# A decoder step on one core: single-group pairs as two chains of two in PSUM, and the gmlp operands stored unsplit

## The chip, the cores and the metric

The kernel runs on one core of a Trainium2 chip. The metric is the device time of one execution in microseconds (us). The engines are TensorE (PE in the profile), VectorE (DVE), ScalarE (ACT), GpSimd (POOL) and SyncE (SP). Here SP issues all loads and stores of data, in the order in which they stand in its program.

## The reference

One layer of a hybrid decoder trunk, for a sample group of 8 sequences of 8 tokens and a prompt of 1024 tokens, which share the weights (D_MODEL 1024, D_FF 2816, float32):

```
h = rmsnorm(x, norm_mix)
q, k, v, gu, gv, ga, gb = split(h @ w_in)
o  = sliding-window attention of 128 with sinks          # sample: cached keys and values
vn = layernorm(gelu(gv));  s = gelu(gu) * (tril(W_s[g]) @ vn + b[g])   # 6 groups of 128 channels
merged = sigmoid(ga) * (o @ w_pa) + sigmoid(gb) * (s @ w_pb)
x = x + merged @ w_out
z = rmsnorm(x, norm_ffn) @ w_up;  c = causal conv of width 3 over z
x = x + (gelu(c_a) * c_b) @ w_down;  y = rmsnorm(x, norm_final)
```

## The kernel before

**Tiling.** Tokens lie on the free axis, in two groups: g0 has the 64 sample tokens and 512 of the prompt (576), g1 the other 512. A float32 value is kept as a high and a low part (`split`: a cast on ACT, line 40, and a subtraction on DVE, line 41), and a product of weight and token is three matmuls: high by high, low by high, high by low.

**Seven products in place of eight.** The input projection (line 282, in the first part of the program) and the up projection (the same line, later) take weight tiles in pairs, cut both in 2 by 2 blocks, and form the outputs by Winograd's form of Strassen's scheme: seven block products of 12 matmuls each, over 288 columns for g0 and 256 for g1. `Chain.product(j, w)` forms one for one group. Products 0, 2, 4 and 6 accumulate on one another in one PSUM bank (name "a"), 1 and 3 in a second ("d"), 5 alone in a third ("c"): the string "adadaca". After some products `keep` copies the state of the bank to SBUF on ACT (line 263 for k and ku, line 265 for kn, which is negated), before the next matmul may write that bank. The four output blocks come from these copies: `put` (line 270) on DVE or POOL, and line 300 on ACT for the last.

**Pairs for one group or for both.** The input projection walks 19 pairs: three for g0 alone, 13 for both groups, three for g1 alone, from 115 to 467 us. In a pair for both groups, each product of g0 is followed by that of g1, so a copy of one group's bank has the other's 12 matmuls beside it. In a pair for one group, it has only the product that stands between two of the bank's own. The up projection (824 to 1298 us) begins with three pairs for g0 alone (f = 0, 1, 2; `FEW` is 3), while DVE, ACT and POOL still finish the token operands: `rstd_last` forms the 1/rms of the second norm and `t1_pieces` hands out twelve pieces (`first`, `second`, `third`, for four blocks each), one after each product from the fifth on. A piece normalises a block, adds or subtracts blocks and splits them.

**Weights.** Class `W` loads weights, adds up the sums that the scheme wants (s1 to s4) and splits them a few units ahead of PE, in the order in which the products take them.

**The gmlp operands.** From 340 us on, jobs (`mix_first`, `mix_job`) are handed out between products. A job for a block of 128 channels loads the normalised v, multiplies it by W_s on PE (line 747 for 128 rows, line 741 for the 64 sample rows of g0), adds the bias, multiplies by gelu(u), splits (tile `sx`) and stores both halves to `sd_` in DRAM. `load_s` (line 796) brings them back into SBUF as tiles `s`, g0 in the last three pairs, g1 behind them. The sample attention and the branch product `s @ w_pb` (line 228) then run from 467 to 500 us, then attention and the branch of the prompt, the output projection (690 to 824 us), the up projection, the down projection (line 1550, to 1536 us) and the last norm. `stage` is a set of four buffers of [128, 576] that loads and jobs share.

**Order.** A scheduler orders the instructions of each engine from the program and its dependences; each engine then runs its instructions in that order, and waits on semaphores.

Of the kernel before, what the change touches and what calls it, by code (L numbers as in the profile page):

```python
# [6 lines left out]
F32 = mybir.dt.float32  # L7
F32R = mybir.dt.float32r
# [7 lines left out]
P = 128  # L16
D = 1024
KD = 8
# [16 lines left out]
def layer(tc, a):  # L35
# [11 lines left out]
    with ExitStack() as top:  # L47
# [22 lines left out]
        class Weights:  # L70
# [4 lines left out]
            def __init__(self, pool, raws, slots):  # L75
# [5 lines left out]
                self.sm = None  # L81
# [5 lines left out]
            def add_pair(self, a_, b_):  # L87
                self.units += [(len(self.items), j) for j in range(7)]
                self.items.append(((a_, b_), KD, None))
# [69 lines left out]
            def total(self, name):  # L159

                if name not in self.sums:
# [4 lines left out]
                    t = self.sm.tile([P, 4, P], F32, name="ws", bufs=2)  # L166
# [85 lines left out]
        class Chain:  # L252


            def __init__(self, g, tx, ps, keeps, places):
                self.g, self.n2, self.tx = g, (288, 256)[g], tx[g]
                self.ps, self.keeps, self.places = ps, keeps, places
                self.bank, self.kept = {}, {}
# [13 lines left out]
            def product(self, j, w):  # L272
                name = "adadaca"[j]
# [55 lines left out]
        sd_ = [[dr(f"sd{g}{c}", [P, 2, n]) for c in range(NG)] for g, n in ((0, 576), (1, 512))]  # L329
# [10 lines left out]
        with ExitStack() as ph1:  # L340
# [50 lines left out]
            for (kind, c, d), _ in seq:  # L391
                W.add_pair(wt(a_tiles[kind][0] + c), wt(a_tiles[kind][1] + d))
# [7 lines left out]
            for f in range(NPRE):  # L400
                for j in range(7):
                    W.add_pre(upd[f][j], 4)
            for f in [*range(NPRE, FEW), *order]:
                W.add_pair(wt(UP0 + f), wt(UP0 + NFF + f))
# [314 lines left out]

            mixin = {}  # L720

            def mix_load(i):
                if i < 2 * NG:
                    g, c = i // NG, i % NG
                    gr, n = groups[g], groups[g]["n"]
                    vn = late["mp"].tile([P, 5, P], F32, name="vn", bufs=2)[:, :len(gr["toks"])]
                    nc.sync.dma_start(vn, vnd[g][:, c])
# [4 lines left out]
            def mix_job(g, c):  # L732
                def go():
# [5 lines left out]
                    if has_s:  # L739
                        ps = psa.tile([P, 512], F32, name="mx", bufs=1)  # L740
                        PE.matmul(ps[:, 0:NS], vn[0:NS, 0], late["wss"][:, c, :], start=True, stop=True)
                        V.tensor_add(t[:, 0:NS].rearrange("p (b t) -> p b t", t=8),
                                     ps[:, 0:NS].rearrange("p (b t) -> p b t", t=8),
                                     bsc[:, :, 0:8].to_broadcast([P, 8, 8]))
                    ps = psa.tile([P, 512], F32, name="mx", bufs=1)
                    for i in range(4):
                        PE.matmul(ps[:, P * i:P * i + P], vn[:, i + has_s], late["wst"][:, c, :],  # L747
# [3 lines left out]
                    V.tensor_mul(t, t, gu)  # L751
# [6 lines left out]
            lns += [mix_first, none, none, lambda: mix_load(0), none] + [mix_job(g, c) for g in range(2) for c in range(NG)]  # L758
# [35 lines left out]
            def load_s(g, pool, c):  # L794
                x = pool.tile([P, 2, groups[g]["n"]], F32R, name=f"s{g}{c}")
                nc.sync.dma_start(x.bitcast(F32), sd_[g][c])
                ss[g].append((x[:, 0], x[:, 1]))

            def prepare_samples():
# [30 lines left out]
                s0 = [lambda c=c: load_s(0, m0, c) for c in range(NG)]  # L830
                return [samples, kt(0), *s0[0:4], kt(1), *s0[4:6], vc(0)]
# [36 lines left out]
            for at, (pair, gs) in enumerate(seq):  # L868
                if at == FEWA + 6:
                    qko.close()  # L870
                if at == len(seq) - FEWA:
# [8 lines left out]
                    (zs[g][e][:, n2 * half:n2 * half + n2], 0, n2),)) for g in gs]  # L880
# [29 lines left out]
            for c in range(NG):  # L910
                load_s(1, m1, c)

            sgs = {}

            def sg_load(c):
# [868 lines left out]
```

## Time and profile before

| | |
|---|---|
| three runs | 1545.92, 1553.11 and 1550.41 us, median 1550.41 |
| profiled execution | 1549.17 us, of which the span of the trace is 1547.4 |
| mean granted TensorE clock | 0.996 of full speed |
| PE busy | 1526.7 us, 99% of the span |
| DVE, ACT, POOL busy | 1177.2, 867.3, 257.6 us |
| HBM traffic | 200.93 MB read, 94.26 MB written |

A row of the timeline gives the start, the duration, the engine, the line, the operation, the tiles (output from inputs), the shape, and in brackets the idle time of the engine before it with what ended it. Matmuls overlap, so what one costs is read from start to start: in undisturbed stretches 0.13 us for 288 columns and 0.11 to 0.12 us for 256, though each shows 0.28 to 0.30 us. A row of the waits gives what an engine waited for: us in all, times, the longest. A row of the groups gives the busy time, the mean duration in ns, and the idle time before. A row of the windows gives the length of a stretch, the busy time and number of instructions of each engine, the granted clock, the share of DMA time and GB/s.

### The profile page before, as it was taken

To read this page: it belongs to the slowest core of one execution; us is meant where nothing else is said; L and a number is where in the kernel's file an instruction comes from. 1 tells how busy PE (TensorE), PEld (TensorE's weight loads), DVE (VectorE), ACT (ScalarE), POOL (GpSimd) and SP (SyncE) were. 2 spreads that over 40 slices of the span, in tenths; PEclk is the share of its full clock that TensorE was granted. 3 is DMA by queue.
4 is the path that set the end of the run, shared out by engine and by line. 5 is a ranking of instruction groups with operands and counts; after the bars stand their busy time and mean duration, and the time that the engine had idled before them with its cause. 6 is when DMAs were issued, how large, how long until landed. Compare 5 with 4: busy or idle time off the path is not lost.

```text
span 1547.4 us, 30111 instructions
## 1 busy us (share of the span) xinstructions
PE 1526.7 (99%) x11532; PEld 1481.1 (96%) x11532; DVE 1177.2 (76%) x1912; ACT 867.3 (56%) x1800; POOL 257.6 (17%) x373
## 2 busy tenths in 40 slices
PE   9999999999999999999999999999999999999997
PEld 9999999999997989988989999999999999999997
DVE  6688776686665885989677878898898878785675
ACT  7557666884554774764444555555555556353452
POOL 0000000011020221320234222332142222000002
PEclk9999999999999999999999999999999999999999
DMA  7687346567789737649977333332332217973453
GB/s 246 207 265 254 137 159 218 190 214 242 265 284 320 232 122 232 218 143 307 333 257 254 127 116 115 120 118 93 107 131 95 106 56 242 355 234 89 135 163 128
DMA packets 134431, 295.19 MB, mean 191 GB/s; under 512 B 15376, under 2 KB 35280, under 8 KB 134288
## 3 DMA queue, kind: packets, MB, share of 16 engines
q1 hardware_dynamic: 134144, 293.27, 56.4%
q8 instruction: 90, 1.47, 0.4%
q14 instruction: 53, 0.43, 0.1%
q10 hardware_dynamic: 144, 0.01, 0.0%
HBM read 200.93 MB, written 94.26 MB: 191 GB/s over the span
## 4 chain that ended last, share of the span: by engine, by line
PE 84%; DMA 7%; DVE 3%; ACT 2%; issue 2%; POOL 1%; SPq 0%; POOLq 0%; DVEq 0%; ACTq 0%
PE st L282 45%; PE mm L228 15%; PE dn L1550 12%; PE st L489 7%; PE sc L1081 2%; PE po L1129 2%; DMA wraw<-wt 1%; PE pt L1108 1%; DVE wl L41 1%; PE mx L747 1%; DMA vnd<-v 1%; DMA s<-sd 1%; DMA q<-qd 0%; DMA kd<-q 0%; DMA wh<-upd 0%
## 5 line engine op out<-in xcount | busy, mean ns | idle before, releaser
L282 PE MATMUL st<-th,wh 128*128 128x288 f32 (+1 forms) x2128 | 615.9, 290 | 5.8 <-ACT k L263 4.7
L282 PE MATMUL st<-tl,wh 128*128 128x288 f32 (+1 forms) x2128 | 613.7, 288 | 0.0
L282 PE MATMUL st<-th,wl 128*128 128x288 f32 (+1 forms) x2128 | 612.5, 288 | 0.0
L282 PEld LDWEIGHTS st<-th,wh 128*128 128x128 f32 x2128 | 403.2, 189 | 8.0 <-ACT k L263 5.6
L282 PEld LDWEIGHTS st<-th,wl 128*128 128x128 f32 x2128 | 403.2, 190 | 0.0
L282 PEld LDWEIGHTS st<-tl,wh 128*128 128x128 f32 x2128 | 402.7, 189 | 0.0
L40 ACT CAST wh<-wraw 128x512 fp32r<-128x512 f32 (+2 forms) x210 | 143.1, 693 | 107.6 <-PE mm L228 36.3
L41 DVE TENSOR_TENSOR wl<-wraw,wh 128x512 fp32r<-128x512 f32 (+2 forms) x210 | 164.2, 794 | 25.7 <-ACT wh L40 23.4
L1550 PE MATMUL dn<-th,wh 128*128 128x288 f32 (+1 forms) x616 | 178.0, 289 | 1.6 <-DVE x L1560 1.6
L1550 PE MATMUL dn<-tl,wh 128*128 128x288 f32 (+1 forms) x616 | 177.7, 288 | 0.0
L1550 PE MATMUL dn<-th,wl 128*128 128x288 f32 (+1 forms) x616 | 177.6, 288 | 0.0
L40 ACT CAST wh<-ws 128x512 fp32r<-128x512 f32 x168 | 102.7, 622 | 88.1 <-PE st L282 67.4
L41 DVE TENSOR_TENSOR wl<-ws,wh 128x512 fp32r<-128x512 f32 x168 | 114.8, 694 | 39.6 <-ACT wh L40 38.8
L1550 PEld LDWEIGHTS dn<-th,wh 128*128 128x128 f32 x616 | 116.4, 189 | 1.8 <-issue 1.3
L1550 PEld LDWEIGHTS dn<-th,wl 128*128 128x128 f32 x616 | 116.6, 189 | 0.0
L1550 PEld LDWEIGHTS dn<-tl,wh 128*128 128x128 f32 x616 | 116.4, 189 | 0.0
L270 POOL TENSOR_TENSOR z<-kn,k 128x288 f32<-128x288 f32 (+1 forms) x32 | 29.4, 920 | 408.6 <-ACT kn L265 391.8
L40 ACT CAST th<-traw 128x544 fp32r<-128x544 f32 (+1 forms) x85 | 54.6, 643 | 53.7 <-PE dn L1550 35.1
L489 PE MATMUL st<-w2h,hh 128*128 128x256 f32 x288 | 81.6, 285 | 0.5 <-ACT rst L455 0.4
L489 PE MATMUL st<-w2l,hh 128*128 128x256 f32 x288 | 81.3, 283 | 0.0
L489 PE MATMUL st<-w2h,hl 128*128 128x256 f32 x288 | 80.8, 284 | 0.0
L41 DVE TENSOR_TENSOR tl<-traw,th 128x544 fp32r<-128x544 f32 (+1 forms) x85 | 61.4, 727 | 25.2 <-ACT th L40 25.2
(266 smaller groups left out, 2936.2 us busy)
## 6 DMA issues: line engine op xcount, KB each, us to landing
wraw<-wt SPq DMA_DIRECT2D x137, 512.0 KB
traw<-td SPq DMA_DIRECT2D x77, 272.0 KB
td<-za SPq DMA_DIRECT2D x22, 544.0 KB
wraw<-wt SPq DMA_DIRECT2D x35, 256.0 KB
q<-qd SPq DMA_DIRECT2D x16, 512.0 KB
upd<-hl SPq DMA_DIRECT2D x14, 512.0 KB
td<-t SPq DMA_DIRECT2D x11, 544.0 KB
qd<-q SPq DMA_DIRECT2D x8, 576.0 KB
```

Of the source, the lines that this page charges most:

```text
L40: S.copy(hi, src)
L41: V.tensor_sub(lo, src, hi.bitcast(F32))
L228: PE.matmul(ps[:, lo:lo + c1 - c0], u[:, k, :], v[:, c0:c1], start=(k == 0 and i == 0), stop=(k == nk - 1 and i == 2))
L270: op(to, pick(x, to, lo, hi), pick(y, to, lo, hi))
L282: PE.matmul(ps, u[:, kk, :], v, start=first and kk + i == 0, stop=kk == 3 and i == 2, skip_group_check=True)
L489: PE.matmul(ps, u[:, lo:lo + P], v[:, k, :], start=k + i == 0, stop=k == KD - 1 and i == 2)
L747: PE.matmul(ps[:, P * i:P * i + P], vn[:, i + has_s], late["wst"][:, c, :], start=True, stop=True)
L1081: PE.matmul(ps[:, h, o0:256], q, kst[kv][:, e, k0:cur + P], start=e == 0, stop=e == 1)
L1108: PE.transpose(pt[:, h * P:h * P + P], s[:, h, 0:P], ident)
L1129: PE.matmul(po, v[:, kv, :], t, start=e == 0, stop=e == len(parts) - 1)
L1550: PE.matmul(place(m, e), u[:, m, :], v[:, lo:hi], start=new and i + k == 0 and (e == 0 or m % 2 == 0), stop=i == NU - 1 and k == 2, skip_g ...
```

## The change

**Single-group pairs** (six of the input projection, three of the up projection) take the products in the order 0, 1, 4, 2, 3, 6, 5 with banks "adbadbc": 0 and 2 accumulate in "a", 1 and 3 in "d", 4 and 6 in "b". Two products of other banks now stand between the two of a bank. The sum that product 4 held before is formed by one more POOL subtraction of two copies, and the last output block by one DVE instruction from PSUM and a copy (it was ACT). The sums s2 and s4 of such a pair overwrite s1 and s2.

**gmlp operands.** `sd_` holds one float32 value. The job no longer splits; the split is done when a block comes back, into the tiles `s` (g0 within the last three pairs, g1 in six parts of the branch). The loads go two ahead through `stage`. The branch takes its pieces in the order (c, g) = (0,0), (1,0), (0,1), (1,1), then by c. The six 64-row matmuls of the sample are done at once (`mix_samples`).

**Start of the up projection.** `rstd_last` is cut in two (`rstd_cols` after the first product, `rstd_rows` after the second), the four scalings of the identity go from ACT to DVE, the pieces start two products earlier, and `second` is cut in two (`second`, `sums`), so there are 16.

**End.** The last norm's sums for (group 1, first half) go after the first m of the second half; the squares of that second half are no longer added up on DVE but enter as further one-column matmuls.

```diff
@@ class Chain @@
             def product(self, j, w):
-                name = "adadaca"[j]
+                name = ("adbadbc" if self.spread else "adadaca")[j]
+                if self.spread:
+                    j = SPREAD[j]
...
                 elif j == 2:
                     self.keep("u", ps)
+                    if self.spread:
+                        G.tensor_sub(kept["n"], kept["n"], kept["u"])
+                        self.put(1, 1, G.tensor_sub, kept["n"], kept["5"])
...
                 elif j == 4:
                     self.keep("n", ps, -1.0)
-                    self.put(1, 1, G.tensor_sub, kept["n"], kept["5"])
+                    if not self.spread:
+                        self.put(1, 1, G.tensor_sub, kept["n"], kept["5"])
...
+                elif self.spread:
+                    for to, lo, hi in self.places(1, 0):
+                        V.scalar_tensor_tensor(to, pick(ps, to, lo, hi), -1.0, pick(kept["u"], to, lo, hi),
+                                               ALU.mult, ALU.subtract)
@@ mix jobs and loads @@
+            def mix_samples():
+                mp = late["mp"]
+                late["sm"] = mp.tile([P, NG, NS], F32, name="sm")
+                ps = psa.tile([P, 512], F32, name="mx", bufs=1)
+                for c in range(NG):
+                    if c % 3 == 0:
+                        v = stage(3 * P)[:NS].rearrange("p (c k) -> p c k", c=3)
+                        nc.sync.dma_start(v, vnd[0][0:NS, c:c + 3, 0])
+                    PE.matmul(ps[:, NS * c:NS * c + NS], v[:, c % 3], late["wss"][:, c, :], start=True, stop=True)
...
-                    sx = mp.tile([P, 2, 576], F32R, name="sx")[:, :, :n]
-                    split(sx[:, 0], sx[:, 1], t)
-                    nc.sync.dma_start(sd_[g][c], sx.bitcast(F32))
+                    nc.sync.dma_start(sd_[g][c], t)
...
-            def load_s(g, pool, c):
+            def load_s(g, c):
+                if c < NG:
+                    s_raw[c] = stage(groups[g]["n"])
+                    nc.sync.dma_start(s_raw[c], sd_[g][c])
+
+            def split_s(g, pool, c):
                 x = pool.tile([P, 2, groups[g]["n"]], F32R, name=f"s{g}{c}")
-                nc.sync.dma_start(x.bitcast(F32), sd_[g][c])
+                split(x[:, 0], x[:, 1], s_raw.pop(c))
@@ branch @@
+            b_order = [(0, 0), (1, 0), (0, 1), (1, 1)] + [(c, g) for c in range(2, KD) for g in range(2)]
...
+                        if i < 2:
+                            at = 3 * i + k0 // 2
+                            split_s(1, m1, at)
+                            load_s(1, at + 2)
@@ start of the up projection @@
+            for i in range(4):
+                V.tensor_scalar(nacc[:, i * P:i * P + P], ident, rt[:, i:i + 1], None, ALU.mult)
+        def rstd_rows():
             rs = psu.tile([P, 512], F32, name="st")
             for i in range(4):
-                S.activation(nacc[:, i * P:i * P + P], ident, AF.Copy, scale=rt[:, i:i + 1])
                 PE.matmul(rs[:, i * P:i * P + P], ones, nacc[:, i * P:i * P + P], start=True, stop=True)
...
-                if f == 0 and j == 2:
-                    rest = t1_pieces(rstd_last())
-                if rest and 7 * f + j > 3:
+                if f == j == 0:
+                    rstd_cols()
+                if f == 0 and j == 1:
+                    rest = t1_pieces(rstd_rows())
+                if rest and 7 * f + j > 1:
                     rest.pop(0)()
@@ end @@
-                        sqs.append(square(0, 1, m, e, False, m < 3 - e))
-                fin[2 + e] = fin_rms(1, e, sqs[3 - e:])
+                        sqs.append(square(0, 1, m, e, False, m < 3 and not e))
+                last = sqs[3 * (1 - e):]
+            fin[3] = fin_rms(1, 1, last)
...
+SPREAD = (0, 1, 4, 2, 3, 6, 5)
```

Three places of the order. First ACT in the third of the g0 pairs at the start of the up projection (th are the splits of token blocks that the pieces make, wh those of weights, k, kn and ku the copies of banks out of PSUM). Before:

```order
L40 CAST th_10662<-traw 128x512
L40 CAST th_10687<-traw 128x512
L263 COPY k_10919<-st 128x288
L40 CAST wh<-ws 128x512
L263 COPY k_10943<-st 128x288
L40 CAST th_10709<-traw 128x512
L263 COPY ku<-st 128x288
```

After:

```order
L40 CAST th_10630<-traw 128x512
L40 CAST wh<-ws 128x512
L40 CAST wh<-wraw 128x512
L269 COPY k_10917<-st 128x288
L40 CAST wh<-wraw 128x512
L40 CAST th_10656<-traw 128x512
L269 COPY k_10940<-st 128x288
L40 CAST th_10677<-traw 128x512
L271 ACTIVATE kn<-st 128x288
```

The first copy of the pair (k_10919, now k_10917) stood behind the casts of two third pieces and now stands behind one.

Second, PE in the sample attention and the branch (mm is the branch product; its operands of 320 and 256 columns are g0's blocks, those of 512 columns g1's; pt and po are transposes of the sample attention). Before:

```order
L228 MATMUL mm<-s_6248,wl 128x320
L228 MATMUL mm<-s_6248,wl 128x256
L228 MATMUL mm<-s_6368,wh 128x512 x2
L228 MATMUL mm<-s_6368,wl 128x512
L1024 MATMUL pt<-c_ident,s_6399 128x128 x4
L1026 MATMUL po<-c_ident,s_6399 64x128 x4
L228 MATMUL mm<-s_6370,wh 128x512 x2
```

After:

```order
L233 MATMUL mm<-s_6245,wl 128x320
L233 MATMUL mm<-s_6245,wl 128x256
L233 MATMUL mm<-s_6004,wh 128x320
L233 MATMUL mm<-s_6004,wh 128x256
L233 MATMUL mm<-s_6004,wh 128x320
L233 MATMUL mm<-s_6004,wh 128x256
```

Behind the last block of g0 for the first output tile there now stands the first block of g0 for the second output tile (s_6004); g1's first block comes 40 rows further down.

On SP, the six loads of g1's operands (s from sd) stood in a row behind the last store of gate values (sg1d from z). Before:

```order
L789 DMA sg1d_136<-z_6203 128x512
L824 DMA cache<-cv 128x1024
L138 DMA wraw<-wpb 128x768
L796 DMA s_6368<-sd_178 128x1024
L796 DMA s_6370<-sd_179 128x1024
L796 DMA s_6372<-sd_180 128x1024
L796 DMA s_6374<-sd_181 128x1024
L796 DMA s_6376<-sd_182 128x1024
```

After:

```order
L825 DMA stg<-sd_178 128x512
L140 DMA wraw<-wpb 128x768
L815 DMA sg1d_135<-z_6028 128x512
L825 DMA stg<-sd_179 128x512
L815 DMA sg0d_127<-z_6027 128x512
L140 DMA wraw<-wpb 128x768
L825 DMA stg<-sd_180 128x512
L140 DMA wraw<-wpb 128x768
L140 DMA wraw<-wpb 128x768
L815 DMA sg1d_136<-z_6182 128x512
```

The first three of them are now ahead of that store and half as large; the other three stand behind the loads of keys and queries of the prompt's attention.

More of the change, by code (lines that the diff above doesn't have):

```diff
@@ L85, in add, with add_pair @@
                 self.items.append(((src,), k, dest))
-            def add_pair(self, a_, b_):
-                self.units += [(len(self.items), j) for j in range(7)]
+            def add_pair(self, a_, b_, spread=False):
+                if spread:
+                    self.in_place.add(len(self.items))
+                self.units += [(len(self.items), j) for j in (SPREAD if spread else range(7))]
                 self.items.append(((a_, b_), KD, None))
@@ L165, in total @@
                             "s4": lambda: (self.total("s2"), a12), "s3": lambda: (a11, a21)}[name]()
-                    t = self.sm.tile([P, 4, P], F32, name="ws", bufs=2)
+                    if name in ("s2", "s4") and self.units[self.emitted][0] in self.in_place:
+                        t = x
+                    else:
+                        t = self.sm.tile([P, 4, P], F32, name="ws", bufs=2)
                     V.tensor_add(t, x, y)
@@ L400, in layer @@
             for f in range(NPRE):
-                for j in range(7):
+                for j in SPREAD:
                     W.add_pre(upd[f][j], 4)
+            early = set(range(NPRE, FEW))
             for f in [*range(NPRE, FEW), *order]:
-                W.add_pair(wt(UP0 + f), wt(UP0 + NFF + f))
+                W.add_pair(wt(UP0 + f), wt(UP0 + NFF + f), f in early)
+                early.discard(f)
             half_p, half_q = order[1::2], order[0::2]
@@ L739, in go @@
                     if has_s:
[L740 to L744, printed above, removed]
+                        V.tensor_mul(t[:, 0:NS], late["sm"][:, c], gu[:, 0:NS])
                     ps = psa.tile([P, 512], F32, name="mx", bufs=1)
                     for i in range(4):
-                        PE.matmul(ps[:, P * i:P * i + P], vn[:, i + has_s], late["wst"][:, c, :],
+                        PE.matmul(ps[:, P * i:P * i + P], vn[:, i], late["wst"][:, c, :],
                                   start=True, stop=True)
@@ L909, in layer, with sg_load @@
             m1 = mo[1].enter_context(tc.tile_pool(name="mlp1", bufs=1, reuse_waits="tile"))
[L910 to L915, printed above, removed]
-                for g in range(2) if c < KD else ():
+            b_order = [(0, 0), (1, 0), (0, 1), (1, 1)] + [(c, g) for c in range(2, KD) for g in range(2)]
+            sgs, bst = {}, {}
+            def sg_load(i):
+                if i < len(b_order):
+                    c, g = b_order[i]
                     n, off = groups[g]["n"], groups[g]["off"]
@@ L1158, in layer @@
             sg_load(0)
-            attention(groups[0], [x for c in range(KD) for x in branch(c)])
+            load_s(1, 0)
+            load_s(1, 1)
+            attention(groups[0], [x for i in range(2 * KD) for x in branch(i)])
             actp.append(right(bo[1], "act1"))
@@ L1406, in third @@
                 t1(kk, 3, 5, t[:, 2:4])
-            return [lambda f=f, kk=kk: f(kk) for f in (first, second, third) for kk in range(4)]
+            steps = [(first, kk) for kk in range(4)] + [(second, 0)]
+            for kk in range(1, 4):
+                steps += [(second, kk), (sums, kk - 1)]
+            steps += [(sums, 3)] + [(third, kk) for kk in range(4)]
+            return [lambda f=f, kk=kk: f(kk) for f, kk in steps]
         def side_loads(f):
@@ L1423, in z_parts, with up_chain @@
             return ((z[:, lo:lo + n2], 0, n2),)
[L1425 to L1426 removed]
+        def up_chain(g, za, zb, spread=False):
+            return Chain(g, tx, psu, up, lambda e, half: z_parts((za, zb)[e], g, half), spread)
         def conv(i, z):
@@ L1688, in layer @@
                         mm_dn(m, e, NU - 4 + x, got[x], False)
-                    if m == 1 and e > 0:
+                    if e and m == 0:
+                        fin[2] = fin_rms(1, 0, last)
+                    elif e and m == 1:
                         fin_mul(1, 0, fin_rb(*fin[2]))
```

62 lines of the change are left out of this document (36 added, 26 removed).

## The prediction

> **What bounds the kernel now.** I read the page first, its busy times, and then what PE waited for.
>
> ```profile
> PE 1526.7 (99%) x11532; PEld 1481.1 (96%) x11532; DVE 1177.2 (76%) x1912; ACT 867.3 (56%) x1800; POOL 257.6 (17%) x373
> ```
>
> ```profile
> PE st L282 <- ACT k L263: 4.7, 3, 2.4
> PE mm L228 <- DMA s<-sd: 1.8, 2, 1.1
> PE dn L1550 <- DVE x L1560: 1.6, 2, 1.3
> PE st L282 <- ACT kn L265: 1.1, 1, 1.1
> PE fs L1585 <- DVE acc L1572: 0.6, 1, 0.6
> ```
>
> PE sets the end: of the span of 1547.4 us it is idle for 20.7 (1547.4 less 1526.7). The change leaves PE's products as they are, so it can win only idle time, time at a lower clock, and small breaks between matmuls. The waits on copies by ACT (k, kn), those on s from sd, and the last row are in its reach; that of L1550 is not. The timeline gives the places: the last matmul before each wait, and the one that started late.
>
> ```profile
> 135.66 0.29 PE L282 MATMUL st<-th,wl 128*128 128x288 f32 x1
> 137.08 0.40 PE L282 MATMUL st<-th,wh 128*128 128x288 f32 x1 [1.12 <-ACT kn L265]
> ...
> 449.25 0.28 PE L282 MATMUL st<-th,wl 128*128 128x256 f32 x1
> 450.50 0.38 PE L282 MATMUL st<-th,wh 128*128 128x256 f32 x1 [0.98 <-ACT k L263]
> ...
> 852.34 0.30 PE L282 MATMUL st<-tl,wh 128*128 128x288 f32 x1
> 852.47 0.29 PE L282 MATMUL st<-th,wl 128*128 128x288 f32 x1
> 855.19 0.61 PE L282 MATMUL st<-th,wh 128*128 128x288 f32 x1 [2.42 <-ACT k L263]
> 855.59 0.45 PE L282 MATMUL st<-tl,wh 128*128 128x288 f32 x1
> 855.83 0.45 PE L282 MATMUL st<-th,wl 128*128 128x288 f32 x1
> ```
>
> These three lie in pairs for one group, at the start and the end of the input projection and at the start of the up projection. The other 1.3 us of waits on k (4.7 less 2.42 and 0.98) lie in a pair for both groups and stay.
>
> **The change part by part.**
>
> *Copies of banks.* A plain step between matmuls of 288 columns is 0.13 us (852.34 to 852.47), so a product of 12 lasts 1.6. Before, a copy that the next user of its bank waits for has one such product of cover; after, two, 3.2 us (for 256 columns at 0.115, 1.4 and 2.8). What makes the copies late is what stands ahead of them in ACT's queue, here three casts (two left out) that run one behind the other from 135.06 on:
>
> ```profile
> 135.06 0.62 ACT L672 CAST th<-stg 128x512 fp32r<-128x512 f32 x1 [1.30 <-DMA stg<-t1d]
> ...
> 136.62 0.40 ACT L265 ACTIVATE kn<-st 128x288 f32<-128x288 f32 x1
> ```
>
> At 137.08 PE is 1.42 us behind its last start, 1.29 more than a plain step; one more product (1.6) covers that: between 0 and -1.3, I take -1.1, near the whole, as the queue of casts may move a little. At 450.50 it is 1.25, 1.13 more than plain, and 1.4 of new cover: 0 to -1.1, I take -0.9.
>
> *Start of the up projection.* The largest wait: at 855.19, 2.72 after 852.47, so 2.59 lost. ACT shows why:
>
> ```profile
> 853.28 0.62 ACT L40 CAST th<-traw 128x512 fp32r<-128x512 f32 x1 [1.02 <-DVE traw L1405]
> 854.22 0.62 ACT L40 CAST th<-traw 128x512 fp32r<-128x512 f32 x1 [0.32 <-DVE traw L1405]
> 854.74 0.39 ACT L263 COPY k<-st 128x288 f32<-128x288 f32 x1
> ```
>
> The copy stands behind two casts of third pieces, which wait for DVE, and DVE is full in that stretch (3.50 of 3.50 us in the windows below). After, it stands behind one such cast, the pieces start two products earlier (some 2 x 1.6 = 3.2 us), and its cover is a product longer. Walking DVE's queue with the durations of before, I find the copy done about 853.4 and PE wanting that bank about 853.8: 0.4 us to spare, in a walk that is no better than 1 us. Bounds: 0 (all of it goes to a longer wait for the pieces, 4 more products of DVE work notwithstanding) and -2.6; I take -2.4.
>
> What is new there: POOL's sum of squares is the last input of `rstd_cols`, and PE would now ask for it right after product 0.
>
> ```profile
> 824.41 1.29 POOL L1252 TENSOR_TENSOR nacc<-nacc,stg 128x512 f32<-128x512 f32 x1 [1.67 <-ACT stg L1251]
> 824.14 2.81 PE st L282 x22
> ```
>
> POOL ends at 825.70. Product 0 starts at about 824.0 and lasts 1.6, so PE asks at about 825.6 and waits 0.1 to 0.5 us: I take +0.3. Behind it PE's whole queue waits, but nothing else does.
>
> *The clock.* After the wait of 2.42 us the matmuls step at 0.24 (855.59 to 855.83), not 0.13:
>
> ```profile
> 851.40:854.90 3.50, 1.36 (x11) 1.13 (x9) 3.50 (x9) 2.16 (x6) 0.00 (x0) 1.00 0.32 124
> 854.90:858.40 3.50, 3.21 (x13) 3.21 (x14) 3.50 (x8) 1.77 (x4) 0.34 (x2) 0.51 0.13 50
> ...
> 1500.00:1503.40 3.40, 3.40 (x18) 3.40 (x17) 3.40 (x11) 3.40 (x9) 0.00 (x0) 0.51 0.31 86
> ```
>
> After a window with 1.36 us of PE work comes one at a granted clock of 0.51: 13 matmuls at some 0.11 more, 1.4 us, at most half the window, 1.7. The last row is the same behind the wait of L1550, which the change leaves. If the wait at 855 goes, its slow window goes: 0 to -1.7, I take -1.1, since a rest of the wait may still bring it.
>
> The Trainium skill, in "TensorE: Matmul & The Clock Gate", Part 1, says that the clock falls to half after at least one idle window of about 3.4 us. This trace shows it after a gap of 2.42 us with 1.36 us of work in the window, so a shorter one was enough here. By the rule the slow window would not belong to this gap and would come again elsewhere, and the sum would be 1.1 less.
>
> *gmlp operands.* Twelve splits leave the jobs and come back at the loads:
>
> ```profile
> L40 ACT CAST sx<-stg x12: 621/650/677, 358.1 to 427.6; 128x576 fp32r<-128x576 f32 x6, 128x512 fp32r<-128x512 f32 x6
> L41 DVE TENSOR_TENSOR sx<-stg,sx x12: 684/722/760, 358.8 to 428.4; 128x576 fp32r<-128x576 f32 x6, 128x512 fp32r<-128x512 f32 x6
> ```
>
> That is 12 x 0.65 = 7.8 us on ACT and 12 x 0.72 = 8.7 on DVE, from a stretch where PE has no waits to one with this load:
>
> ```profile
> 455.00:475.00 20.00, 20.00 (x171) 18.19 (x169) 9.49 (x14) 11.55 (x23) 1.64 (x2) 1.00 0.91 329
> 475.00:500.00 25.00, 23.16 (x146) 18.93 (x145) 13.39 (x34) 8.31 (x29) 1.08 (x4) 1.00 1.03 327
> ```
>
> From 455 to 500 us alone DVE has 22.1 us free (45 less 9.49 and 13.39) and ACT 25.1, so the free time of these two hides the splits and I put them at nothing; without it each would cost PE up to 0.65 + 0.72. DMA is full from 455 on, and there the change loads half: six operands of 576 and six of 512 KB become half as large, 3.3 MB less, some 10 us of that traffic at 327 GB/s. The waits that this can take away:
>
> ```profile
> 478.96 0.74 PE L228 MATMUL mm<-s,wh 128*128 128x512 f32 x2 [1.13 <-DMA s<-sd]
> ```
>
> ```profile
> 470.16 2.92 DMA sg1d<-z
> 473.48 7.93 DMA s<-sd
> ```
>
> The last two rows are of the chain that ended last: SP issued s behind the store sg1d, at 473, and they took 7.93 us. After, three of the six loads of g1 stand ahead of that store, and PE first takes g0's second output tile. Bounds: -1.8 (both waits), and with the splits late a loss, priced below. I take -1.6, near the whole, for the loads come earlier and are wanted later.
>
> *The 64-row matmuls.* Six breaks in PE's stream become one.
>
> ```profile
> 354.14 0.28 PE L282 MATMUL st<-th,wl 128*128 128x256 f32 x1
> 354.35 0.43 PE L741 MATMUL mx<-c_wss,vn 64*128 64x64 f32 x2
> 354.71 0.40 PE L282 MATMUL st<-th,wh 128*128 128x288 f32 x1
> 354.95 0.29 PE L282 MATMUL st<-tl,wh 128*128 128x288 f32 x1
> ```
>
> From 354.14 to 354.95 pass 0.81 us. Two plain steps of 0.12 and 0.13 and the two small ones, taken at 0.13 each, make 0.51; the other 0.30 is the break. Five fewer: -1.5 at most, 0 at least, I take -1.1, since the two loads that the one visit waits for may split it.
>
> *The rest.* Nine more POOL subtractions (0.92 us each) and a DVE instruction per pair instead of one on ACT lie off PE's path: POOL is busy for 17% of the span, and the last block is wanted a pair later.
>
> ```profile
> L270 POOL TENSOR_TENSOR z<-kn,k 128x288 f32<-128x288 f32 (+1 forms) x32 | 29.4, 920 | 408.6 <-ACT kn L265 391.8
> 1536.91 0.58 PE L1585 MATMUL fs<-c_ones,acc 128*128 128x1 f32 x4 [0.57 <-DVE acc L1572]
> ```
>
> At the end PE waits 0.57 us for a DVE sum that goes, and gets two more sets of one-column matmuls: 0 to -0.6, I take -0.4.
>
> *Sum:* -1.1 - 0.9 - 2.4 + 0.3 - 1.1 - 1.6 - 1.1 - 0.4 = -8.3 us. The profiled execution took 1549.17, so 1540.9; it lies 1.2 below the median of 1550.41, from which the same sum gives 1542. All best bounds together make -10.5 (1.3 + 1.1 + 2.6 - 0.1 + 1.7 + 1.8 + 1.5 + 0.6).
>
> **The rivals.** *The waits move instead of going.* For it: ACT's and DVE's queues are fixed in order, DVE is full around 850, and my slack there is 0.4 us. If half of the 855 wait stays (-1.2), the clock falls again (0) and the new operands wait as long as the old did (0), the sum is -1.1 - 0.9 - 1.2 + 0.3 - 1.1 - 0.4 = -4.4: 1546.
>
> *Slower: g1's operands come late.* The last three of g1's loads each want a stage buffer that a split sets free, and stand behind the loads of keys and queries. The first such split is at about 472, since its cast is behind the last sigmoid on ACT. Two round trips follow (buffer, load, split of 0.65 + 0.72), and PE wants the last block at about 491, by its queue of 72 matmuls for g0, 15 for g1 and the sample's own. So a load may take up to (491 - 472 - 2.8)/2 = 8.1 us. The row of 7.93 is close to that, though it is six loads of 512 KB at once. Above 8.1 every us costs two, ACT's casts hold up the copies and exponentials behind them, and PE's gap would bring a slow window of 1.5. The gain of the rest is 6.7, so from 10.7 us on the kernel is slower (2 x 2.6 + 1.5); at 16, twice the row, it is 15.8 + 1.5 - 6.7 = +10.6: 1561. Against it: half the bytes, and three loads are early.
>
> *More than the sum:* if every bound comes out best (-10.5) and the wait of L1550 falls so that the window behind it, at 0.51 now, keeps the full clock (1.5), -12: 1538.4. Against it: nothing at that wait is changed.
>
> **How the numbers follow.** The forecast gets 0.55, with a range of its own of 1540 to 1545; moved waits 0.27, late operands 0.09, more 0.09. The bound of 0.5%, about what a measurement here can tell from no change, is 7.75 us, so 1542.7. The forecast is just beyond it; I give two thirds of it to faster, 0.36, and with "more" 0.45. Slower by 0.5% are most of the late operands, 0.07; the rest, 0.48, is within. The range of 1537 to 1550 takes in the moved waits and "more", with 1.5 to 4 us on either side for the spread of the runs shown, and leaves out the late operands.
>
> **What would show it.** Right: no wait on k or kn in the three first and three last input pairs; the windows around 855 without 0.51; no wait on the s operands at L228's new place; one visit of the 64-row matmuls. Wrong: a wait of PE on ACT's k copy near 850; ACT's casts of s waiting on DMA stg from sd between 475 and 490 with PE idle behind them; a wait of over 0.5 us at `rstd_cols`. The forecast falls if these waits are gone and the time is not, or if a stretch untouched by the change shows new idle time.

## The result

| kernel | median, us | runs | ratio to before, 95% interval |
|---|---|---|---|
| before | 1549.23 (1545.92 to 1553.11) | 6 | |
| changed | 1541.33 (1539.93 to 1542.81) | 6 | 0.995 (0.9933 to 0.9968) |

The change is 7.9 us faster (1549.23 less 1541.33); 8.3 were forecast, and a median of 1542 against the measured 1541.33. The profiled execution of the changed kernel took 1540.46 us with a span of 1538.2, 9.2 less than that of before. The line of busy times of its page, and what PE waited for (what, us in all, times, longest):

```profile
PE 1523.1 (99%) x11540; PEld 1479.5 (96%) x11540; DVE 1178.5 (77%) x1927; ACT 863.1 (56%) x1784; POOL 269.8 (18%) x382
```

```profile
PE dn L1607 <- DVE x L1617: 1.3, 3, 0.8
PE sc L1123 <- DMA q<-qd: 1.2, 1, 1.2
...
PE st L290 <- ACT k L269: 1.0, 2, 0.7
PE fs L1657 <- DVE dg L1649: 1.0, 1, 1.0
PE sc L1036 <- issue: 0.8, 1, 0.8
```

The waits on s and on kn are gone, those on k are down from 4.7 to 1.0. New are 0.8 us ahead of the sample's scores (sc L1036), and the wait on q is 1.2 where it was 0.3. In the third g0 pair of the up projection the timeline now shows 0.37 us between two starts where 2.72 stood, and the windows (length, busy times, clock) no slow one:

```profile
849.76 0.29 PE L290 MATMUL st<-th,wl 128*128 128x288 f32 x1
850.13 0.40 PE L290 MATMUL st<-th,wh 128*128 128x288 f32 x1
```

```profile
846.50:850.00 3.50, 3.50 (x27) 3.32 (x25) 3.50 (x10) 1.91 (x5) 0.17 (x1) 1.00 0.26 100
850.00:853.50 3.50, 3.43 (x26) 3.38 (x26) 3.50 (x8) 2.45 (x6) 0.17 (x1) 1.00 0.53 150
```

Both kernels issue the same number of matmuls into st (7326), mm (1588) and dn (1848). So the start of the same one can be compared between traces, which gives where the time went. The table does that against the first trace of before, stretch by stretch, for three more traces: a second one of before and two of the changed kernel (both repeats are told of below).

| stretch, us of before | before again | changed | changed again |
|---|---|---|---|
| start, to 66 | +0.3 | +0.3 | 0.0 |
| first three pairs, to 151 | +0.2 | -1.4 | -1.4 |
| to 340, holds the wait at 322 | -0.5 | -0.6 | -1.1 |
| gmlp jobs, to 438 | +0.1 | -1.9 | -1.9 |
| last three pairs, to 467 | -1.1 | +0.5 | +0.6 |
| sample attention and branch, to 524 | +0.2 | -1.8 | -1.8 |
| to 617, holds the wait on q | +0.1 | +1.0 | +0.5 |
| to 824 | 0.0 | 0.0 | 0.0 |
| start of the up projection, to 884 | -1.1 | -4.0 | -4.0 |
| to 1471 | 0.0 | 0.0 | 0.0 |
| down projection, to 1515 | -2.6 | -1.6 | -1.8 |
| to the last dn matmul, 1536 | 0.0 | -0.2 | -0.3 |
| behind it | 0.0 | +0.6 | +0.4 |
| all | -4.4 | -9.2 | -10.8 |

The second column is the lesson of the table: the same kernel, traced again, is 4.4 us shorter. The waits at 322, 450, 597 and 1497 us and the slow windows come and go by themselves. What can be put down to the change are the stretches in which both traces of it agree, and both of before to 0.3 us: the first pairs, the gmlp jobs, the sample attention, the end of the down projection. The start of the up projection is one too, once the slow window that only the first trace of before has there is set aside.

### The profile page after: what moved, and what is told of

Its sections match the earlier page's. It is cut to its first block, busy times and chain, and to the rows that moved or that the text cites. A ratio compares the mean times of both kernels' runs of the same rounds, so it can differ in the third digit from the quotient of the medians.

```text
span 1538.2 us, 30167 instructions
## 1 busy us (share of the span) xinstructions
PE 1523.1 (99%) x11540; PEld 1479.5 (96%) x11540; DVE 1178.5 (77%) x1927; ACT 863.1 (56%) x1784; POOL 269.8 (18%) x382
## 4 chain that ended last, share of the span: by engine, by line
PE 87%; DMA 4%; DVE 4%; issue 2%; ACT 2%; POOL 1%; SPq 0%; POOLq 0%; DVEq 0%; ACTq 0%
PE st L290 47%; PE mm L233 16%; PE dn L1607 11%; PE st L507 6%; PE sc L1123 2%; PE po L1171 2%; DMA wraw<-wt 1%; DVE wl L41 1%; PE pt L1150 1%; PE mx L775 1%; DMA q<-qd 1%; DVE tl L41 0%; DMA v<-gvd 0%; DMA vnd<-v 0%; DMA x<-xt 0%
## 5 line engine op out<-in xcount | busy, mean ns | idle before, releaser
L271 ACT ACTIVATE kn<-st 128x256 f32<-128x256 f32 (+1 forms) x76 | 30.0, 396 | 75.3 <-PE st L290 75.2
```

The costliest lines, as they stand in the source:

```text
L271: S.activation(t, src, AF.Copy, scale=by)
```

## The experiments

**The kernel before again.**

> The kernel before, one more trace of it. It had a window at a granted clock of 0.51 behind the waits at 855 and at 1497 us, of 3.4 us each, worth 1.4 to 1.5 us each. Theory 'gap': each such wait brings its slow window in every execution, so both are there again. Rival 'phase': the windows run free of the program and a wait counts only where it falls well into one; then one or both are missing in this trace, which is shorter by 1.4 us for each. The two waits themselves (2.4 and 1.3 us) are there in any case.

It took 1544.81 us in this execution, its span is 1543.1. Its windows around the wait of the third g0 pair:

```profile
850.90:854.40 3.50, 1.34 (x11) 1.10 (x9) 3.50 (x9) 2.04 (x6) 0.00 (x0) 1.00 0.43 167
854.40:857.90 3.50, 3.50 (x27) 3.50 (x28) 3.50 (x8) 3.14 (x7) 0.34 (x2) 1.00 0.02 7
```

The wait is there (1.34 us of work in this stretch of 3.50, as before), the slow window is not: "phase". (These rows are cut around the wait, not along the windows of the clock; those follow under *The clock*.) At 1497 us, too, the time lost ahead of the first late matmul is 0.26 where it was 1.40, so waits vary as well as windows.

**The sample's 64-row matmuls at once, alone.**

```diff
+            def mix_samples(): ...            # as in the change
-                        PE.matmul(ps[:, 0:NS], vn[0:NS, 0], late["wss"][:, c, :], start=True, stop=True)
+                        V.tensor_mul(t[:, 0:NS], late["sm"][:, c], gu[:, 0:NS])
```

> The kernel before with one part of the change alone: the six 64-row matmuls of the sample at one visit. The changed kernel won 1.9 us between 340 and 437 us. Theory 'breaks': five breaks of 0.30 go, -1.2 to -1.6 us in that stretch. Rival 'splits': what won there is the twelve splits that left ACT and DVE in that stretch; then this kernel shows only 0 to -0.7. In the total of some 1548 us this is at the edge of what can be told; the stretch is read from the trace.

1545.0 us against 1550.06, ratio 0.9968 (0.9954 to 0.9982). The stretch of the gmlp jobs is 1.94 us shorter, to the hundredth what the changed kernel shows, with the splits still in the jobs. Theory "breaks" holds, and "splits" falls. The one visit in the changed kernel:

```profile
340.45 0.28 PE L290 MATMUL st<-th,wl 128*128 128x256 f32 x1
340.65 1.55 PE L747 MATMUL mx<-c_wss,stg 64*128 64x64 f32 x12
342.13 0.40 PE L290 MATMUL st<-th,wh 128*128 128x288 f32 x1
342.37 0.30 PE L290 MATMUL st<-tl,wh 128*128 128x288 f32 x1
```

From 340.45 to 342.37 pass 1.92 us for what took six times 0.81. Less the plain steps of its neighbours (0.12 + 0.13) that is 1.67 against six times 0.56 = 3.36: 1.69 of the 1.94. The other 0.25 is the first visit of the 128-row matmuls: between the products around it pass 1.41 us before and 1.14 here. The total of this kernel gained more (5 us) than this stretch. In its trace the wait at 450 was not there, as in the second trace of before, and one at 138 us was longer (2.23); what the other 3 us of the total are from stays open.

**The early pieces alone.** The kernel before with `rstd_cols`, `rstd_rows`, the 16 pieces and their start, nothing else.

> The kernel before with one part of the change alone: the 1/rms in two halves and the sixteen pieces two products earlier. Theory 'early': the wait on k of 2.1 to 2.6 us in the third g0 pair of the up projection falls to about 1.3, as where the changed kernel keeps the old order there: -0.8 to -1.3 us in that stretch, without slow windows. Rival 'all needed': the weights' sums and splits come at other times than in the changed kernel, and the wait stays above 2.

1547.54 against 1550.01, ratio 0.9981 (0.9971 to 0.9991).

```profile
856.33 0.40 PE L282 MATMUL st<-th,wh 128*128 128x288 f32 x1 [1.13 <-ACT k L263]
```

The wait is 1.13 us where three traces with the late pieces and the old order had 2.42, 2.2 and 2.0: theory "early".

**The up projection without the new order.**

```diff
-            ch = up_chain(0, za, zb, True)
+            ch = up_chain(0, za, zb, False)     # and the weights' units in the old order
```

> The changed kernel, but with the old order of products and one chain of four in the three g0 pairs at the start of the up projection (the pieces still start two products earlier). Theory 'cover': the second product between the uses of a bank is what took the wait of 2.42 us away, so without it PE waits for an ACT copy of k by 1 to 2.4 us in the third of these pairs, with or without a slow clock window behind it (1.4): 1 to 4 us more than the changed kernel from the start of the up projection to its next pair. Rival 'early': the two products' head start of the pieces (3.2 us) is enough by itself, no wait above 0.3 us, within 0.5 us of the changed kernel.

1539.83 against 1550.06, ratio 0.9933 (0.9912 to 0.9955): in the total not to be told from the changed kernel. In the trace:

```profile
847.57 0.29 PE L290 MATMUL st<-th,wl 128*128 128x288 f32 x1
849.01 0.40 PE L290 MATMUL st<-th,wh 128*128 128x288 f32 x1 [1.15 <-ACT k L269]
```

```profile
848.04 0.62 ACT L40 CAST th<-traw 128x512 fp32r<-128x512 f32 x1 [1.06 <-DVE traw L1456]
848.57 0.39 ACT L269 COPY k<-st 128x288 f32<-128x288 f32 x1
```

The copy of k is again behind a third piece's cast that waits for DVE, and PE waits 1.15 us: 1.1 us longer than the changed kernel in this stretch (-2.8 against -4.0). "Cover" is right by the trace, at the low end of its range.

**The new order without the early pieces.**

```diff
-                if f == j == 0:
-                    rstd_cols()
-                if f == 0 and j == 1:
-                    rest = t1_pieces(rstd_rows())
-                if rest and 7 * f + j > 1:
+                if f == 0 and j == 2:
+                    rest = t1_pieces(rstd_last())     # as before
+                if rest and 7 * f + j > 3:
```

> The changed kernel, but with the 1/rms and the twelve pieces as before (first piece at the fifth product, second pieces uncut, identity scaled on ACT); the two chains of two stay. Theory 'cover': 1.6 us of new cover against a wait of 2.59: about 1.0 us of wait on k stays, 1 to 2.5 us more than the changed kernel in this stretch. Theory 'early': the pieces' own lateness sets the wait, so it stays whole or moves to a later product: 2.4 us or more, and a slow window behind it. If cover alone is enough: no wait, and 0.1 us less than the changed kernel, since the wait on the sum of squares goes.

1546.83 against 1550.06, ratio 0.9978 (0.9965 to 0.9991). The stretch is 4.1 us longer than in the first trace of before, 8.1 longer than in the changed kernel, some 2.9 of it in two slow windows:

```profile
851.82 0.40 PE L290 MATMUL st<-th,wl 128*128 128x288 f32 x1 [1.79 <-DVE wl L41]
854.54 0.51 PE L290 MATMUL st<-th,wh 128*128 128x288 f32 x1 [1.12 <-ACT wh L40]
855.76 0.61 PE L290 MATMUL st<-th,wl 128*128 128x288 f32 x1 [0.48 <-DVE wl L41]
```

```profile
850.75 0.42 DVE L1449 SCALAR_TENSOR_TENSOR traw<-traw,x1g 128x256 f32<-128x256 f32 x1
851.08 0.69 DVE L41 TENSOR_TENSOR wl<-ws,wh 128x512 fp32r<-128x512 f32 x1
```

A fourth wait, of 1.09 us on ACT's kn, stands at 842.86, in the second pair. "Early" has the size (2.4 us or more, at a later product, with slow windows behind), but neither theory has the place: the wait doesn't stay on k, most of it moves to the weights. DVE is full with pieces and runs them one behind the other, and the split of a weight (851.08) is now what comes late. So the new order needs the early pieces; without them it makes this stretch longer, in the one trace there is. By the waits: neither 2.0 to 2.4 us, early alone 1.1, both 0.2 at most, the new order alone 3.4 in the three places shown and 1.1 in the fourth.

**The input projection without the new order**, all else as changed.

```diff
-                W.add_pair(wt(a_tiles[kind][0] + c), wt(a_tiles[kind][1] + d), len(gs) == 1)
+                W.add_pair(wt(a_tiles[kind][0] + c), wt(a_tiles[kind][1] + d), False)
```

> The changed kernel, but with the old order and one chain of four in the six single-group pairs of the input projection. Theory 'cover': the waits on kn at 137 (1.1 us) and on k near 450 (1.0) come back, and the wait of 0.8 ahead of the first scores goes, as the last product is another: +1.4 in the first three pairs, and 0 to +1 from 437 us to the first scores. Rival: in the last three pairs the added splits and the POOL subtractions are what holds the copies up, so the wait near 450 is larger than before, 1.5 us or more.

1541.41 against 1549.53, ratio 0.995 (0.9936 to 0.9964): in the total not to be told from the changed kernel. In the trace:

```profile
PE st L290 <- ACT k L269: 2.4, 2, 1.7
...
PE st L290 <- ACT kn L271: 0.9, 1, 0.9
```

The wait on kn is back (first three pairs -0.07 against -1.42), and no wait stands ahead of the first scores. The wait near 450 is the longest of all traces, 1.7, as the rival had it. But that wait isn't tied to the splits: with the old order and no moved split it was 0.98 in the first trace of before and absent in the second.

**The new order in the first three pairs alone** (and in the up projection).

```diff
-                W.add_pair(..., len(gs) == 1)
+                W.add_pair(..., gs == (0,))
```

> The changed kernel, with two chains of two only in the three g0 pairs of the input projection and in the up projection; the last three pairs (g1) have the old order. Theory: in the last three pairs two chains of two cost more than they win: the waits of 0.5 (456 us) and 0.8 to 1.0 (first scores) go, the wait near 450, which comes and goes with either order, may be there (0 to 1.9): -1.4 us to +0.5 against the changed kernel between 437 us and the first scores. Rival: the wait near 450 is there in every execution with the old order, at 1 us or more.

1540.39 against 1550.01, ratio 0.9935 (0.992 to 0.995), again not to be told from the changed kernel. The waits at 456 and ahead of the scores are gone, the wait near 450 is there (1.2): from 438 us to the first scores +1.2 against the first trace of before, the changed kernel +0.5 and +0.6. That is 0.6 to 0.8 worse in this trace, not better, and beyond the theory's +0.5. Over all traces, what is lost at the wait near 450 beyond a plain step was 1.1, 0, 0, 1.9, 1.4 and 1.0 us with the old order in these pairs (mean 0.9), and 0, 0, 0, 1.2, 0, 0, 1.0 and 0.6 with the new one (mean 0.35). So it comes with both, and the rival, by which it is there with the old order in every execution, falls too; that it is less with the new order isn't settled by so few traces.

**The bank of the first scores.** In the changed kernel, PE and then DVE at the end of the input projection:

```profile
462.69 0.28 PE L290 MATMUL st<-th,wl 128*128 128x256 f32 x1
463.78 0.44 PE L1036 MATMUL sc<-cache,qs 128*64 128x128 f32 x4 [0.81 <-issue]
```

```profile
462.38 0.96 DVE L41 TENSOR_TENSOR wl<-wraw,wh 128x768 fp32r<-128x768 f32 x1 [0.30 <-ACT wh L40]
463.26 0.41 DVE L276 TENSOR_TENSOR z<-k,st 128x256 f32<-128x256 f32 x1
```

The profile names no releaser ("issue"). But DVE's read of the last product's bank, held up by a weight's split, ends at 463.67, 0.11 ahead of the first scores. Two edits place the scores in other banks:

```diff
# pools_swapped
-            psm = ...tile_pool(name="psm", bufs=1, space=PSUM...)
             pmm = ...tile_pool(name="pmm", bufs=2, space=PSUM...)
+            psm = ...tile_pool(name="psm", bufs=1, space=PSUM...)
# pt_first
+            for x in ("pt", "po"):
+                psm.tile([P, 512], F32, name=x)
```

> The changed kernel, but the PSUM pool of the branch products is opened ahead of the pool of the attention's scores, so the first scores of the sample no longer lie in the bank of the input projection's last product, which DVE still reads. Theory 'bank': the new wait of 0.81 us ahead of the first scores (463 us) is DVE's reading of that bank; it goes, -0.5 to -0.9 us there. Rival: the wait is that of the cache or of the scores' operands (a load, POOL), and it stays at 0.8.

> The changed kernel, but in the PSUM pool of the sample attention the tiles pt and po are placed ahead of the scores' tile, so the scores lie two banks further and the branch's pool stays where it is. Theory 'bank': the wait ahead of the first scores goes as with the swapped pools (-0.8 to -1.0 us), and the wait of 0.9 us at the first product of the up projection, which the swap brought, does not come: 0.8 to 1.0 us faster than the changed kernel in the trace. Rival: DVE's later reads are as late for the other bank, and the wait stays.

With the swap:

```profile
461.25 0.28 PE L290 MATMUL st<-th,wl 128*128 128x256 f32 x1
461.45 0.44 PE L1036 MATMUL sc<-cache,qs 128*64 128x128 f32 x4
...
817.64 0.41 PE L290 MATMUL st<-th,wh 128*128 128x288 f32 x1 [0.78 <-DVE x1g L1286]
```

With pt and po first:

```profile
463.34 0.28 PE L290 MATMUL st<-th,wl 128*128 128x256 f32 x1
463.55 0.44 PE L1038 MATMUL sc<-cache,qs 128*64 128x128 f32 x4
```

From the last product to the first scores pass 0.20 and 0.21 us instead of 1.09: "bank" holds. The swap only carries the wait to the next place where a bank changes hands, the first product of the up projection, which now lies in a bank that DVE still reads (0.78). pt_first avoids both. In time: the swap 1539.21 against 1549.53, ratio 0.9939 (0.9927 to 0.9952); pt_first 1539.91 against 1550.01, 0.9933 (0.9917 to 0.9949), beside the changed kernel again:

> The changed kernel once more, beside the two variants sent with it. If the waits at 135 to 137 us and at 850, the 64-row matmuls and the s operands are the lasting part, this trace shows the same steps there (-1.4, about -2.8 without slow windows, -1.9, -1.8) and the wait of 0.8 to 1.0 ahead of the first scores; the waits at 322, 450, 597 and 1490 us, and slow windows, may differ from the first trace by 1 us and more each, as between the two traces of the kernel before.

1540.41 against 1550.01, ratio 0.9938 (0.9922 to 0.9955), and its lasting steps are those of the table. pt_first is 0.5 us faster in the median, which these runs can't tell from nothing; its 0.9 us at the scores shows in the trace alone.

**The gmlp operands as before**, with their jobs, loads and order of the branch; all else as changed.

> The changed kernel, but with the gmlp operands split at the store, loaded as two halves and taken in the old order, and the sample's 64-row matmuls one at a time. Theory 'loads': the waits on s from sd (1.1 and 0.65 us) come back, and the stretch from 340 to 437 us loses its 1.9: together 3 to 4.5 us slower than the changed kernel. Rival 'half comes from elsewhere': without the added splits ACT and DVE are freer in the last three pairs, the waits there (0.5 and 0.8) go, and it is only 1 to 2.5 slower.

1548.74 against 1549.53, ratio 0.9998 (0.9987 to 1.0009): nearly all of the gain is gone, more than either theory gave it. Its trace, of the fastest of its ten executions, is 5.6 us longer than that of the changed kernel. The stretch of the jobs loses its 1.9, as "loads" has it, but the waits on s from sd don't come back: PE waits for none of them. Most of the rest is at the first scores. PE, DVE and ACT there:

```profile
463.30 0.28 PE L290 MATMUL st<-th,wl 128*128 128x256 f32 x1
466.77 0.65 PE L1013 MATMUL sc<-cache,qs 128*64 128x128 f32 x4 [3.20 <-issue]
```

```profile
464.18 0.96 DVE L41 TENSOR_TENSOR wl<-wraw,wh 128x768 fp32r<-128x768 f32 x1 [2.81 <-ACT wh L40]
...
465.39 0.95 DVE L41 TENSOR_TENSOR wl<-wraw,wh 128x768 fp32r<-128x768 f32 x1
466.25 0.42 DVE L276 TENSOR_TENSOR z<-k,st 128x256 f32<-128x256 f32 x1
```

```profile
463.31 1.80 ACT L40 CAST wh<-wraw 128x768 fp32r<-128x768 f32 x2 [3.41 <-DMA wraw<-wpb]
```

The bank's wait of 0.8 is 3.2 us here: a weight is late (ACT waits for its load until 463.31), its split on DVE is late, and the read of the bank stands behind the split. Behind the gap PE runs two windows at half clock (the first four scores take 0.65 us for 0.44). The mean granted clock of the ten executions is 0.993 to 0.995, that of the changed kernel's 0.995 to 0.997, so the other executions seem to have such windows too.

Why the load is late isn't shown. The queue carries twice the bytes of operands; but SP also issues the weights at other times, none between 447.65 and 458.51, where the changed kernel issues one at 454.12. In the first trace of before ACT waits for such a load as well (until 465.79), and PE does not wait at the scores. So it seems that the lateness counts only with the new order, which has put that bank in the way.

**The branch in its old order**, g1's splits all in the first piece.

```diff
-            b_order = [(0, 0), (1, 0), (0, 1), (1, 1)] + [(c, g) for c in range(2, KD) for g in range(2)]
+            b_order = [(c, g) for c in range(KD) for g in range(2)]
```

> The changed kernel, but the branch takes its pieces group by group within an output tile, as before ((0,0), (0,1), (1,0), ...), with g1's six splits all in the three parts of the first piece. Theory 'order': g1's blocks are then wanted some 40 matmuls (5 us) earlier than they come, and PE waits for them 1 to 5 us in all between 470 and 490 us. Rival 'bytes': the halved loads are enough, as the first three are issued early, and the waits stay below 0.5 us in all.

1539.87 against 1549.53, ratio 0.9944 (0.993 to 0.9957). The stretch of the sample attention gains 1.6, nearly the 1.8 of the changed kernel, and no wait on the operands shows: "bytes". The new order of the pieces isn't needed for it. (A wait of 1.6 us on the merge, near 690 us, stands in this trace alone; what it is from was not tried.)

## Why the prediction was right, and where not

*Copies of banks.* At 137 us -1.1 was taken, -1.42 came, in every kernel with the new order there, and -0.1 to +0.7 in three without it (a fourth, the one with the 64-row matmuls alone, had a slow window there). The bound of -1.3 was too tight: it left out the slower second step behind a gap (137.08 to 137.31, 0.1 over plain). Near 450 us -0.9 was taken, and the last three pairs came out at +0.5 and +0.6. Here two steps failed, and so did one of the signs of being right, no wait on k in these pairs. The wait near 450 was read from one trace as belonging to the order of products; it comes and goes with either. And "the last block is wanted a pair later" is not so for the last pair: its last bank is wanted at once by the next pool, for 0.9 us, and a copy at 456 us is late by 0.5 in six of the eight traces with the new order in these pairs.

*Start of the up projection.* -2.4 + 0.3 was taken. The first row of the table has a slow window in this stretch, so the second trace of before is the one to compare with: -4.0 against -1.1, -2.9. Right in kind and near in size; the wait at `rstd_cols` was 0.15 us rather than 0.3. What the sum did not have is how its parts hang together: the early pieces are worth about half, and without them the new order costs.

*The clock.* -1.1 was taken on the reading that a wait brings its slow window. Of four traces with a wait or waits of 2 us and more there, three had one; of the ten with 1.2 us or less, none at that place. So the term was right on average, for a reason only half seen: what decides is how the gap falls into the windows of the clock. In the records of the granted clock every slow stretch within the program lasts 3.41 us or twice that, and the slow stretches of one trace begin whole multiples of 3.41 us apart (in before 854.9 and 1500.0: 189 of them), so the windows ahead of one can be counted back. In before, and then in before again:

```profile
851.51:854.92 3.41, 1.25 (x10) 1.02 (x8) 3.41 (x9) 2.07 (x6) 0.00 (x0) 1.00 0.34 130
```

```profile
850.18:853.59 3.41, 1.99 (x15) 1.74 (x14) 3.41 (x9) 1.85 (x5) 0.00 (x0) 1.00 0.19 74
853.59:857.00 3.41, 2.67 (x20) 2.67 (x21) 3.41 (x7) 2.92 (x7) 0.34 (x2) 1.00 0.27 105
```

In the first trace the gap falls nearly whole into one window, which has 1.25 us of PE work, and the next is slow. In the second a window's edge cuts the gap, the two windows have 1.99 and 2.67 us of work, and none is slow.

The Trainium skill ("TensorE: Matmul & The Clock Gate", Part 1) says that the clock falls to half after at least one idle window of some 3.4 us. Here a gap of 2.42 us, with 1.25 us of work in its window, was enough, and no slow window came elsewhere ahead of the end in the two traces of the changed kernel. That the windows run free of the program, which that part of the Trainium skill also says, agrees with the two traces of before.

*gmlp operands.* -1.6 was taken, -1.8 came. But the reason given, that they come earlier and are wanted later, is half wrong: the later want did nothing. "I put the splits at nothing" holds for PE. Late operands, the rival on the slower side, did not come. The last two loads are issued by SP at 478.14 and 484.39, and ACT takes the last at 486.97:

```profile
478.14 0.32 SPq L825 DMA_DIRECT2D stg<-sd  x1
...
484.39 0.32 SPq L825 DMA_DIRECT2D stg<-sd  x1
```

```profile
486.97 0.62 ACT L40 CAST s<-stg 128x512 fp32r<-128x512 f32 x1 [0.69 <-DMA stg<-sd]
```

A round trip of 2.6 us, far from the 8.1 that it might have taken; PE wants that block at 491.55, by the prediction at about 491.

*The 64-row matmuls.* -1.1 was taken with a bound of -1.5; -1.94 came. The break was sized from two steps at 0.30. Six visits of two small matmuls cost 0.56 us each and one of twelve 1.67, both without the steps of the neighbours: that makes 0.11 for a small matmul and 0.34 for the break, 1.69 for five. The other 0.25, at the first 128-row visit, was not in the sum.

*The rest.* -0.4 was taken for the end. To the last matmul of the down projection -0.25 came, and behind it +0.6 and +0.4. Every trace has a slow window at its end, and where it begins decides: in the ten traces with the new end, +0.3 to +0.7 where it begins within 3.8 us of that matmul and catches the last small ones (six), -0.2 to -0.3 where it begins after 4.4 us or more (four). That is +0.2 on average, so the end as a whole won nothing.

*Not in the sum:* the wait on q near 597 us (this stretch +1.0 and +0.5, -0.5 to +0.3 in ten other traces and +1.2 in one). The code is the same on either side, but the wait is 0 to 0.4 us in the six traces with the old order in the last three pairs and 0.4 to 1.6 in the eight with the new one. So part of it may belong to that order; nothing was tried on it. The window behind the wait of L1550 was missing in both traces of the changed kernel, but in the second of before too.

With the lasting stretches -1.4, -1.9, -1.8, -2.9 and -0.25, some +0.9 at the end of the input projection (new waits of 0.5 and 0.9 less the 0.5 that the wait near 450 fell by on average), and 1.1 for the slow window, the sum is -8.5. The +0.2 behind the last matmul and some +0.6 for another slow window (last section) make it -7.7; -7.9 and, in the second comparison, -9.6 were measured. That the forecast hit so closely is luck: its misses nearly cancel, +1.8 at the last three pairs against -0.3 at the first, -0.8 at the 64-row matmuls, -0.8 at the start of the up projection and -0.2 at the operands.

By the medians alone the parts can't be added up like this. With the old order back in the up projection (1539.83), in all six input pairs (1541.41) or in the last three (1540.39) the time is that of the changed kernel (1541.33 and 1540.41), with intervals of 2 to 3 us either way: what the new order wins shows in traces only. The one visit of the 64-row matmuls gains 5.1 us by itself, the early pieces 2.5, and without the gmlp part nearly all is lost. The new order, the end and the unsplit operands were not run alone.

## What to carry to other kernels

Before a wait in a trace is put on the account of an order, look at a second trace of the same kernel: here five waits moved by 1 us and more, and slow windows came and went, with no edit at their place, as much as most terms of the sum. When an operation goes to another engine or a bank rotation gets another length, follow the last bank of the stage to the pool that takes it over, not only the block that it feeds. And two edits that free the same queue should be tried apart and together: of the order and the early pieces each looked like the cure, and one of them alone made it worse.

## What the runs showed of the hardware

A window of half clock can come without any gap in PE's busy time. In a trace of pt_first:

```profile
820.60:824.00 3.40, 3.40 (x28) 3.33 (x28) 0.95 (x5) 0.66 (x2) 0.01 (x1) 0.99 0.98 254
824.00:827.40 3.40, 3.40 (x17) 3.40 (x16) 1.26 (x3) 0.72 (x2) 0.33 (x1) 0.50 0.90 313
```

In the first row PE is busy for all 3.40 us, but 16 of its matmuls are the one-column ones of `rstd_cols`, from 820.67 to 822.4. Four of the ten traces with the early `rstd_cols` have this window, none of the four with `rstd_last`. With the windows counted back as above in all fourteen, nine have 15 or 16 of the one-column matmuls in one window. In four of the nine 9 to 11 other matmuls stand beside them, and these are the four with the slow window; in the other five it is 12 to 14, and the next window is fast. In the remaining five traces a window's edge cuts the 16, with at most 13 on one side, and none is slow. So it is again a matter of how the work falls into the windows. That one-column matmuls count as little work fits this; no edit tried it. With a cost of about 1.45 us in 4 of 10 traces it takes an estimated 0.6 from the change.

And a visit of 64-row matmuls between two products cost 0.34 us beyond the steps of its own matmuls, though no wait shows.
